# Expert search of two PEER layers issued in shares per slab behind the low parts, with GpSimd's low parts and the gate steps placed differently

## The chip, the cores and the metric

One core of one Trainium2 chip runs the whole kernel in one launch. Times are device microseconds (us). The engines are TensorE (PE, weight loads PEld), VectorE (DVE), ScalarE (ACT), GpSimd (POOL) and SyncE (SP, which issues the loads). The time before is the median of three runs, 2640.13 us (2637.69 to 2642.39).

## The reference, cut to what matters

Eight stages follow each other over 256 tokens of width 1024, all in float32: an MLA mixer, a PEER layer, a DSA mixer, a second PEER layer, and two pairs of hybrid mixer and SwiGLU. Each ends in a layernorm. The change is in the two PEER layers:

```python
q = (xt @ w_q).reshape(T, PEER_HEADS, 2, PEER_QDIM // 2)
s1 = jnp.einsum('thd,hnd->thn', q[:, :, 0], sub_keys[0])
s2 = jnp.einsum('thd,hnd->thn', q[:, :, 1], sub_keys[1])
v1, i1 = lax.top_k(s1, PEER_TOPK)
v2, i2 = lax.top_k(s2, PEER_TOPK)
cand = (v1[..., :, None] + v2[..., None, :]).reshape(T, PEER_HEADS, 256)
best, pos = lax.top_k(cand, PEER_TOPK)
expert = jnp.take_along_axis(cand_idx, pos, axis=-1)
gate = jax.nn.softmax(best, axis=-1)
# per token, over its 8 * 16 experts:
a = x . w_down[expert];  hg = gelu(a) * gate;  y = sum(hg * w_up[expert])
```

Eight heads each choose 16 of 128 x 128 = 16,384 experts.

## The kernel before, in words

The kernel gathers no expert rows. It multiplies all tokens with all 16,384 rows of w_down, slab by slab (128 slabs of 128 experts, loop at L959), takes Gelu, multiplies by a gate that is zero for experts that were not chosen, and multiplies the result H with all of w_up (128 slabs, L992).

*Products in parts.* A float32 product is made of three fp32r products. `Stream._split` (L55 to L71) takes each loaded weight tile of 128 x 1024, `raw`, in the order of a written plan; ScalarE makes the high part `whi` (L67), and VectorE, or GpSimd where the plan's third field says so, the low part `wlo` = raw - high (L69). `raw` has four buffers, the parts have three. `Stream.get` for slab k makes the parts up to k + 2 and so lets their loads go out. `mmS` (L191 to L193) then issues 24 matmuls per slab: for each of eight blocks high x high, high x low of x, and low x high. In the plan the odd peer_down slabs under 40 and every fourth one after that have their low part made by GpSimd, 42 of 128 in each layer.

*The search.* While the slabs run, `route()` (L872) works out the choice on VectorE. `keys_of` finds the 16 best of 128 keys per head, side and token half with five instructions (`topk16`, L761: max, max_index, match_replace, max, max_index). `experts_of` builds 54 candidate sums per head (L782) and finds the 16 best of those. `select` (L804) makes the gates: subtract the best, Exp on ScalarE, sum, reciprocal, normalise (L813). `keys16` (L821) turns positions into key numbers with one-hot comparisons and sums of 16-bit numbers (L840 to L843). `to_hk` (L790) transposes the results on PE and writes them, twice over, into IG.

*What sets the order.* The work is written as a generator in `self.bg`, and `tick` advances it by one yield: twice per pair of query slabs (L907), once per down slab (L976). That is only the order in which the program is traced: the scheduler behind Tile (L1356) may move an instruction ahead on its engine when its data is ready, and each engine then runs a fixed order. Nothing ties the search to the low parts.

*The gates.* When the generator is spent, the routing's memory is given back, H1 is opened, and `gates()` (L924) takes over: for eight tokens at a time four 16-bit one-hot operations on VectorE (L939), then after two steps 16 matmuls (L946), whose sum multiplies the H of finished slabs on VectorE (L951) or is copied into H for later ones on ScalarE (L954). Later slabs then take Gelu into `av` and multiply on GpSimd (L974). 32 groups of two steps make 64 steps, one more before them reads the number row and one after them ends it. `drain` after the loop finishes what is left over.

Of the kernel before, what the change touches and what calls it, by code (L numbers as in the profile page):

```python
# [34 lines left out]
class Stream:  # L35
# [21 lines left out]
    def _split(self, upto):  # L57
        nc = self.nc
        while self.splits <= min(upto, len(self.plan) - 1):
            i = self.splits  # L60
            self._load(i)
            w = self.plan[i][1].shape[-1]
            r = self.raws.pop(i)
            pool = self.tail if self.plan[i][3] else self.spl
            hi = pool.tile([128, 1024], F32R, name="whi")
            lo = pool.tile([128, 1024], F32R, name="wlo")
            nc.scalar.activation(hi[:, :w], r[:, :w], AF.Copy)  # L67
            eng = nc.gpsimd if self.plan[i][2] else nc.vector
            eng.tensor_tensor(lo[:, :w], r[:, :w], hi[:, :w].bitcast(F32), ALU.subtract)  # L69
            self.parts[i] = (hi, lo)  # L70
            self.splits += 1  # L71
            self._load(i + self.nraw)
# [20 lines left out]
def make_plan(I, stages):  # L93
    plan = []

    def add(key, ap, pool=False, tail=False):
        plan.append((key, ap, pool, tail))

    for s in stages:
# [17 lines left out]
        elif s[:4] == "peer":  # L117
# [3 lines left out]
            for k in range(12):  # L121
                add("peer_q", I["peer_q"][l, k])
            for k in range(128):
                add("peer_down", I["peer_down"][l, k], k % (2 if k < 40 else 4) == 1)
            for k in range(128):
                add("peer_up", I["peer_up"][l, k], False, k > 123)
        elif s[:3] == "mix":
# [29 lines left out]
class Build:  # L157
# [591 lines left out]
    def peer(self, l):  # L749
        nc, I, st, tc = self.nc, self.I, self.st, self.tc  # L750
        with ExitStack() as c0:
# [6 lines left out]
            P16 = [rp.tile([128, 8, 16], U32, name=f"P{a}") for a in range(2)]  # L758
            best = rp.tile([128, 2, 8, 16], F32, name="best")

            def topk16(vals, idx, src, w):  # L761
                s2 = rp.tile([128, 128], F32, name="s2", bufs=2)
                nc.vector.max(vals[:, 0:8], src)
                nc.vector.max_index(idx[:, 0:8], vals[:, 0:8], src)
                nc.vector.match_replace(s2[:, :w], vals[:, 0:8], src, FLOOR)  # L765
                nc.vector.max(vals[:, 8:16], s2[:, :w])
                nc.vector.max_index(idx[:, 8:16], vals[:, 8:16], s2[:, :w])  # L767

            def keys_of(hd, ss):
                for a in range(2):  # L770
                    for side in range(2):
                        topk16(V[a][:, side, hd], X[a][:, side, hd], ss[:, side, a, :], 128)
                        yield

            def experts_of(h0, a):

                w = int(CSTART[-1])
                hs = slice(h0, h0 + 4)
                cd = rp.tile([128, 4, w], F32, name="cand", bufs=2)
                for (i, n, m), o in zip(CAND, (int(CSTART[c[0]]) for c in CAND)):  # L780
                    sh = [128, 4, n, m]
                    nc.vector.tensor_tensor(cd[:, :, o:o + n * m].rearrange("p h (i j) -> p h i j", i=n),  # L782
                                            V[a][:, 0, hs, i:i + n, None].to_broadcast(sh),
                                            V[a][:, 1, hs, None, 0:m].to_broadcast(sh), ALU.add)
                for j in range(4):
                    topk16(best[:, a, h0 + j], P16[a][:, h0 + j], cd[:, j], w)
                    if j != 1:
                        yield

            def to_hk(src, j, a):  # L790

# [11 lines left out]

            def select():  # L804

                e = rp.tile([128, 16, 16], F32, name="ge")
                gs = rp.tile([128, 2, 16], F32, name="gs")
                bv = best.rearrange("p a h k -> p (a h) k")
                nc.vector.tensor_tensor(e, bv, bv[:, :, 0:1].to_broadcast([128, 16, 16]), ALU.subtract)
                nc.scalar.activation(e, e, AF.Exp)  # L810
                nc.vector.reduce_sum(gs[:, 0], e, AX.X)
                nc.vector.reciprocal(gs[:, 1], gs[:, 0])
                nc.vector.tensor_tensor(e, e, gs[:, 1, :, None].to_broadcast([128, 16, 16]), ALU.mult)  # L813
                yield
                for a in range(2):
                    to_hk(e[:, a * 8:a * 8 + 8].rearrange("p a b -> p (a b)"), 2, a)
                yield
                for a in range(2):
                    yield from keys16(a)

            def keys16(a):  # L821

# [9 lines left out]
                dx = rp.tile([128, 8, 16], F16, name="dx")  # L832
                nc.vector.tensor_copy(dx[:, :, 0:1], x16[:, 0, :, 0:1])
                tt(dx[:, :, 1:16], x16[:, 0, :, 1:16], x16[:, 0, :, 0:15], ALU.subtract)
                hot = rp.tile([128, 128, 16], F16, name="hot")
                prod = rp.tile([128, 128, 16], F16, name="prod")

                def total(x, out):

                    tt(prod.rearrange("p (h k) i -> p h k i", h=8), hot.rearrange("p (h k) i -> p h k i", h=8), x, ALU.mult)  # L840
                    for n in (8, 4, 2):
                        tt(prod[:, :, 0:n], prod[:, :, 0:n], prod[:, :, n:2 * n], ALU.add)
                    tt(out, prod[:, :, 0:1], prod[:, :, 1:2], ALU.add)  # L843

                lists = lambda x: x[:, :, None, :].to_broadcast([128, 8, 16, 16])
                tt(duo(hot), pos[:, :, None, :].to_broadcast(R), row(1), ALU.is_ge)
                yield
                k1 = rp.tile([128, 128, 1], F32, name="k1")
                total(lists(dx), k1)
                yield  # L850
                first = rp.tile([128, 128, 1], F16, name="first")
                total(self.rows16[:, 2, None, None, :].to_broadcast([128, 8, 16, 16]), first)
                yield
                to_hk(k1.rearrange("p k u -> p (k u)"), 0, a)
                tt(pos, pos, first.to_broadcast([128, 128, 2]), ALU.subtract)
                tt(duo(hot), pos[:, :, None, :].to_broadcast(R), row(0), ALU.is_equal)
                yield
                k2 = rp.tile([128, 128, 1], F32, name="k2")
                total(lists(x16[:, 1]), k2)
                yield  # L860
                yield
                to_hk(k2.rearrange("p k u -> p (k u)"), 1, a)

            def scores_of(hd, qT, ss):
                b = self.acc()
# [6 lines left out]
            def route():  # L872
# [86 lines left out]
            for k in range(128):  # L959
# [5 lines left out]
                if k % 2:  # L965
# [394 lines left out]
```

## Time and profile before

| | us |
|---|---|
| median of three runs | 2640.13 |
| profiled execution, its own time | 2644.85 |
| its span, first to last instruction | 2643.1 |
| PE busy | 2596.4 (98%) |
| DVE busy | 1826.4 (69%) |
| ACT busy | 1366.8 (52%) |
| POOL busy | 433.9 (16%) |

The two peer_down loops lie at 157 to 568 us and 1107 to 1520 us of the span. Busy time of PE is no measure of its speed, since matmuls overlap; the number of matmuls in a stretch is. A slab is 24 matmuls.

### The profile page before, as it was taken

The numbers are of one execution on the slowest core, as the hardware profiler recorded it, in microseconds if no ns is written. First come the engines' busy times: TensorE is split into PE (matmuls) and PEld (weight loads), VectorE is DVE, ScalarE is ACT, GpSimd is POOL, SyncE is SP. The second block draws the span as 40 slices with busy tenths as digits, with TensorE's granted clock in tenths as the row PEclk, the third lists the DMA queues.
The fourth block names the chain that finished last, engine by engine and source line by source line (L and its number), as shares of the span: only waits on it lengthen the run. The fifth ranks groups of instructions, "written<-read, shape, count | busy, mean of one in ns | idle before, by whom it ended". The sixth has DMA issues, their size and how long they took to land.

```text
span 2643.1 us, 44763 instructions
## 1 busy us (share of the span) xinstructions
PE 2596.4 (98%) x17412; PEld 2374.2 (90%) x17412; DVE 1826.4 (69%) x3301; ACT 1366.8 (52%) x2091; POOL 433.9 (16%) x292
## 2 busy tenths in 40 slices
PE   8999999999999999989999999999999999999998
PEld 7899999998888887989999988888899899899898
DVE  6696689956666688885799666666766655666555
ACT  5544454455555555544544455555576444575443
POOL 1024333430000032133234400000101000101000
PEclk9999999999999999999999999999999999999999
DMA  5555545566676655545555566766645666536664
GB/s 196 185 152 165 181 155 159 157 185 193 192 225 195 193 187 176 158 153 172 174 159 153 175 191 193 228 193 192 215 126 177 223 189 208 181 121 207 208 186 141
DMA packets 134213, 477.05 MB, mean 180 GB/s; under 512 B 15568, under 2 KB 17376, under 8 KB 133744
## 3 DMA queue, kind: packets, MB, share of 16 engines
q1 hardware_dynamic: 130016, 459.43, 55.7%
q0 software_dynamic: 3984, 14.76, 1.5%
q8 instruction: 136, 2.23, 0.4%
q14 instruction: 77, 0.63, 0.1%
HBM read 465.74 MB, written 8.39 MB: 179 GB/s over the span
## 4 chain that ended last, share of the span: by engine, by line
PE 70%; issue 15%; DVE 10%; DMA 2%; ACT 1%; POOL 1%; SPq 0%; DVEq 0%; POOLq 0%; ACTq 0%
PE acc L202 20%; PE acc L199 10%; PE wk L191 9%; PE wk L193 9%; PE wk L192 9%; PE acc L946 2%; DVE wlo L69 2%; PE acc L191 2%; PE acc L192 2%; PE acc L193 2%; PE acc L241 1%; DVE xres L353 1%; DVE s L765 1%; DVE X L767 1%; DVE z L362 1%
## 5 line engine op out<-in xcount | busy, mean ns | idle before, releaser
L69 DVE TENSOR_TENSOR wlo<-raw,whi 128x1024 fp32r<-128x1024 f32 (+2 forms) x766 | 947.0, 1240 | 553.0 <-ACT whi L67 541.4
L67 ACT ACTIVATE whi<-raw 128x1024 fp32r<-128x1024 f32 (+3 forms) x854 | 895.4, 1051 | 709.7 <-PE wk L192 346.4
L193 PE MATMUL wk<-xTh,wlo 128*128 128x256 f32 x2880 | 818.5, 284 | 14.7 <-DVE wlo L69 14.7
L191 PE MATMUL wk<-xTh,whi 128*128 128x256 f32 x2880 | 824.4, 286 | 0.0
L192 PE MATMUL wk<-xTl,whi 128*128 128x256 f32 x2880 | 817.0, 284 | 0.0
L193 PEld LDWEIGHTS wk<-xTh,wlo 128*128 128x128 f32 x2880 | 554.7, 193 | 16.5 <-DVE wlo L69 16.1
L191 PEld LDWEIGHTS wk<-xTh,whi 128*128 128x128 f32 x2880 | 554.6, 193 | 2.1 <-ACT whi L67 0.9
L192 PEld LDWEIGHTS wk<-xTl,whi 128*128 128x128 f32 x2880 | 554.9, 193 | 1.4
L202 PE MATMUL acc<-wlo,hgh 128*128 128x512 f32 x1024 | 315.9, 389 | 0.0
L202 PE MATMUL acc<-whi,hgl 128*128 128x512 f32 x1024 | 315.7, 389 | 0.1
L69 POOL TENSOR_TENSOR wlo<-raw,whi 128x1024 fp32r<-128x1024 f32 x88 | 227.3, 2584 | 359.5 <-ACT whi L67 351.2
L199 PE MATMUL acc<-whi,hgh 128*128 128x512 f32 x1024 | 276.0, 389 | 0.0
L254 ACT ACTIVATE hgh<-H 128x256 fp32r<-128x256 f32 x256 | 106.4, 418 | 288.1 <-PE acc L202 288.0
L202 PEld LDWEIGHTS acc<-whi,hgl 128*128 128x128 f32 x1024 | 192.1, 188 | 40.4 <-DVE hgl L255 0.5
L202 PEld LDWEIGHTS acc<-wlo,hgh 128*128 128x128 f32 x1024 | 192.2, 188 | 39.9
L199 PEld LDWEIGHTS acc<-whi,hgh 128*128 128x128 f32 x1024 | 192.1, 188 | 39.9
L255 DVE TENSOR_TENSOR hgl<-H,hgh 128x256 fp32r<-128x256 f32 x256 | 111.8, 439 | 114.6 <-PE acc L202 114.2
L974 POOL TENSOR_TENSOR H<-H,av 128x512 f32<-128x512 f32 (+16 forms) x76 | 103.5, 1361 | 271.1 <-ACT av L973 258.3
L356 POOL TENSOR_TENSOR lsm<-lsm,mhalf 128x1 f32<-128x1 f32 x16 | 9.0, 562 | 838.9 <-DVE lsm L355 484.7
L191 PE MATMUL acc<-xTh,whi 128*128 128x256 f32 x384 | 112.0, 292 | 0.0
L193 PE MATMUL acc<-xTh,wlo 128*128 128x256 f32 x384 | 110.0, 287 | 0.0
L192 PE MATMUL acc<-xTl,whi 128*128 128x256 f32 x384 | 109.1, 284 | 0.0
(412 smaller groups left out, 3442.9 us busy)
## 6 DMA issues: line engine op xcount, KB each, us to landing
raw<-in_peer_down SPq DMA_DIRECT2D x256, 512.0 KB, 3.6
raw<-in_peer_up SPq DMA_DIRECT2D x256, 512.0 KB, 4.2
raw<-in_ffn_down SPq DMA_DIRECT2D x44, 512.0 KB, 4.2
raw<-in_ffn_gate SPq DMA_DIRECT2D x40, 512.0 KB, 4.2
raw<-in_ffn_up SPq DMA_DIRECT2D x40, 512.0 KB, 4.2
raw<-in_peer_q SPq DMA_DIRECT2D x32, 512.0 KB, 4.2
raw<-in_gates SPq DMA_DIRECT2D x32, 512.0 KB, 3.5
raw<-in_dsa_qkv SPq DMA_DIRECT2D x24, 512.0 KB, 4.5
```

What stands on the lines that cost most here:

```text
L67: nc.scalar.activation(hi[:, :w], r[:, :w], AF.Copy)
L69: eng.tensor_tensor(lo[:, :w], r[:, :w], hi[:, :w].bitcast(F32), ALU.subtract)
L191: mm(out, whi[:, sl[k]], xh[:, k, :], start=k == 0, stop=False)
L192: mm(out, whi[:, sl[k]], xl[:, k, :], start=False, stop=False)
L193: mm(out, wlo[:, sl[k]], xh[:, k, :], start=False, stop=k == nk - 1)
L199: mm(o, xh, whi[:, c], start=first, stop=False)
L202: self.last_mm = mm(o, x, w[:, c], start=False, stop=s)
L241: mm(o, xh, w[:, c], start=s, stop=False)
L254: nc.scalar.activation(hi, src, AF.Copy)
L255: nc.vector.tensor_tensor(lo, src, hi.bitcast(F32), ALU.subtract)
L946: nc.tensor.matmul(b[:, j * 128:j * 128 + 128], B[:, 4 * q + j], A[:, 4 * q + j], start=first and j == 0, stop=not first and j == 3)
L974: nc.gpsimd.tensor_tensor(H[j][:, c, :n], H[j][:, c, :n], av[:, :, :n], ALU.mult)
```

## The change

Five edits, all within the two PEER layers.

1. GpSimd makes the low parts of the odd down slabs under 24 only: 12 per layer instead of 42.
2. `_split` remembers the last low part that VectorE makes (`last_lo`).
3. The search yields after every VectorE instruction or a few of them, with a number for its cost. A new function `pace` takes over from `tick`: each call adds a share to the account (1850 while heads and candidates are ranked, 1200 from `select` on, 850 more per call in the query stage) and issues steps until it is used up. All that it issues is placed after `last_lo` on VectorE.
4. The transposes (`to_hk`) are put in a list, `later`, and issued at the fourth call of `pace` counted from the one that made their data, and the gate's normalisation follows the first step of `keys16`.
5. The gates step in every slab but those divisible by 6.

```diff
             eng = nc.gpsimd if self.plan[i][2] else nc.vector
-            eng.tensor_tensor(lo[:, :w], r[:, :w], hi[:, :w].bitcast(F32), ALU.subtract)
+            ins = eng.tensor_tensor(lo[:, :w], r[:, :w], hi[:, :w].bitcast(F32), ALU.subtract)
+            if not self.plan[i][2]:
+                self.last_lo = ins
...
-                add("peer_down", I["peer_down"][l, k], k % (2 if k < 40 else 4) == 1)
+                add("peer_down", I["peer_down"][l, k], k < 24 and k % 2 == 1)
...
             def topk16(vals, idx, src, w):
                 s2 = rp.tile([128, 128], F32, name="s2", bufs=2)
+                cost = 120 + w
                 nc.vector.max(vals[:, 0:8], src)
+                yield cost
                 nc.vector.max_index(idx[:, 0:8], vals[:, 0:8], src)
+                yield cost
...
                 nc.scalar.activation(e, e, AF.Exp)
-                nc.vector.reduce_sum(gs[:, 0], e, AX.X)
-                nc.vector.reciprocal(gs[:, 1], gs[:, 0])
-                nc.vector.tensor_tensor(e, e, gs[:, 1, :, None].to_broadcast([128, 16, 16]), ALU.mult)
-                yield
-                for a in range(2):
-                    to_hk(e[:, a * 8:a * 8 + 8].rearrange("p a b -> p (a b)"), 2, a)
-                yield
-                for a in range(2):
-                    yield from keys16(a)
+                share = 1200
+                yield 400
+                for x in keys16(0):
+                    yield x
+                    if e is not None:
+                        nc.vector.reduce_sum(gs[:, 0], e, AX.X)
+                        nc.vector.reciprocal(gs[:, 1], gs[:, 0])
+                        nc.vector.tensor_tensor(e, e, gs[:, 1, :, None].to_broadcast([128, 16, 16]), ALU.mult)
+                        for a in range(2):
+                            turn(e[:, a * 8:a * 8 + 8].rearrange("p a b -> p (a b)"), 2, a)
+                        e = None
+                        yield 800
+                yield from keys16(1)
+
+            def turn(*args):
+                later.append([4, args])
...
                     tt(prod.rearrange("p (h k) i -> p h k i", h=8), hot.rearrange("p (h k) i -> p h k i", h=8), x, ALU.mult)
+                    yield 1000
                     for n in (8, 4, 2):
                         tt(prod[:, :, 0:n], prod[:, :, 0:n], prod[:, :, n:2 * n], ALU.add)
+                        yield 120 + n * 60
                     tt(out, prod[:, :, 0:1], prod[:, :, 1:2], ALU.add)
+                    yield 250
...
+            search, later, spent, share = route(), [], 0, 1850
+
+            def pace(more=0):
+
+                nonlocal search, spent
+                spent -= share + more
+                with tc.issue_after(st.last_lo.ins):
+                    while search and spent < 0:
+                        c = next(search, None)
+                        if c is None:
+                            search = None
+                        else:
+                            spent += c
+                    for x in later:
+                        x[0] -= 1
+                    while later and later[0][0] <= 0:
+                        to_hk(*later.pop(0)[1])
...
-            self.bg = [route()]
...
                 if hd > 2:
-                    self.tick(2)
+                    pace(850)
...
-                self.tick()
-                if not self.bg and not routed:
+                if routed:
+                    if k % 6:
+                        self.tick()
+                else:
+                    pace()
+                if not routed and not search and not later:
                     routed = True
```

The costs in the steps left out are 130 for a candidate sum, 800 for the start of `keys16`, 1000 for its first comparison and 1300 for its second.

## Rows read from the trace of the kernel before

**Rows 1.** The page, busy time of each engine: us, share of the span, instructions

```profile
PE 2596.4 (98%) x17412; PEld 2374.2 (90%) x17412; DVE 1826.4 (69%) x3301; ACT 1366.8 (52%) x2091; POOL 433.9 (16%) x292
```

**Rows 2.** The table of waits: who <- for whom: us in total, times, longest

```profile
PE wk L193 <- DVE wlo L69: 14.7, 7, 3.0
```

**Rows 3.** Windows: stretch, us, busy PE PEld DVE ACT POOL (instructions), clock, DMA

```profile
163.71:192.51 28.80, 28.80 (x243) 28.80 (x241) 28.80 (x177) 14.30 (x16) 11.27 (x5) 1.00 0.55 165
192.51:228.81 36.30, 28.41 (x219) 27.60 (x217) 36.06 (x91) 14.71 (x17) 12.86 (x5) 0.95 0.42 129
231.69:257.61 25.92, 25.92 (x219) 25.92 (x217) 7.79 (x7) 11.96 (x14) 10.52 (x5) 1.00 0.59 187
453.02:520.09 67.07, 67.07 (x643) 66.64 (x641) 66.90 (x93) 31.27 (x59) 29.87 (x16) 1.00 0.52 157
1142.85:1180.61 37.76, 30.97 (x218) 30.36 (x217) 37.52 (x92) 14.72 (x17) 11.55 (x5) 0.86 0.41 138
```

**Rows 4.** Timeline at a wait of PE, layer 0: start, us, instruction, [idle before]

```profile
190.84 2.39 POOL L69 TENSOR_TENSOR wlo<-raw,whi 128x1024 fp32r<-128x1024 f32 x1 [3.36 <-ACT whi L67]
190.97 2.31 DVE L782 TENSOR_TENSOR cand<-V 128x32 f32<-128x32 f32 x1
193.60 1.21 DVE L69 TENSOR_TENSOR wlo<-raw,whi 128x1024 fp32r<-128x1024 f32 x1
194.87 0.39 PE L193 MATMUL wk<-xTh,wlo 128*128 128x256 f32 x1 [1.96 <-DVE wlo L69]
```

**Rows 5.** Timeline of VectorE in the search, layer 0

```profile
160.11 0.87 DVE L763 MAX8 V<-ss 128x8 f32<-128x128 f32 x4
162.08 0.07 DVE L764 MATCH_VALUE_LOAD X<-V,ss 128x8 f32 x1
162.34 0.07 DVE L764 MATCH_VALUE_LOAD X<-V,ss 128x8 f32 x1
```

**Rows 6.** Search operations by line: ns least/median/most, first to last start

```profile
L766 DVE MAX8 V<-s x64: 268/284/304, 134.3 to 1139.9; 128x8 f32<-128x128 f32 x64
L767 DVE FIND_INDEX8 X<-V,s x64: 278/289/303, 137.7 to 1143.6; 128x8 uint32<-128x128 f32 x64
L782 DVE TENSOR_TENSOR cand<-V x40: 172/196/2308, 141.5 to 1143.8; 128x32 f32<-128x32 f32 x16, 128x40 f32<-128x40 f32 x8, 128x48 f32<-128x48 f32 x8, 128x64 f32<-128x64 f32 x8
```

**Rows 7.** High parts (L67) and low parts (L69) by line

```profile
L67 ACT ACTIVATE whi<-raw x854: 634/1060/1070, 5.5 to 2622.4; 128x1024 fp32r<-128x1024 f32 x168, 128x704 fp32r<-128x704 f32 x2, 128x584 fp32r<-128x584 f32 x1
L69 DVE TENSOR_TENSOR wlo<-raw,whi x766: 681/1225/3417, 6.3 to 2623.5; 128x1024 fp32r<-128x1024 f32 x187, 128x704 fp32r<-128x704 f32 x2, 128x584 fp32r<-128x584 f32 x2, 128x768 fp32r<-128x768 f32 x1
L69 POOL TENSOR_TENSOR wlo<-raw,whi x88: 2383/2406/4478, 154.5 to 1506.7; 128x1024 fp32r<-128x1024 f32 x88
```

**Rows 8.** Timeline of ScalarE around Exp, layer 0

```profile
202.18 1.28 ACT L810 ACT_TABLE_LOAD   x1
206.66 0.42 ACT L810 ACTIVATE ge<-ge 128x256 f32<-128x256 f32 x1 [3.20 <-DVE ge L809]
208.99 1.28 ACT L970 ACT_TABLE_LOAD   x1
```

**Rows 9.** Groups of VectorE, 192.51 to 228.81: xcount | busy us, mean ns

```profile
L813 DVE TENSOR_TENSOR ge<-ge,gs 128x256 f32<-128x256 f32 x1 | 2.6, 2635 | 0.0
L842 DVE TENSOR_TENSOR prod<-prod 128x1024 f16<-128x1024 f16 x3 | 2.0, 680 | 0.0
L842 DVE TENSOR_TENSOR prod<-prod 128x512 f16<-128x512 f16 x3 | 1.2, 415 | 0.0
L840 DVE TENSOR_TENSOR prod<-hot,x 128x2048 f16<-128x2048 f16 x1 | 1.2, 1224 | 0.0
```

**Rows 10.** Gate operations by line: ns least/median/most

```profile
L939 DVE TENSOR_TENSOR A<-io,IG x64: 675/682/2897, 283.0 to 1473.2; 128x1024 f16<-128x1024 f16 x64
L951 DVE SCALAR_TENSOR_TENSOR H<-acc,H x228: 155/396/426, 322.5 to 1483.1; 128x256 f32<-128x256 f32 x102, 128x208 f32<-128x208 f32 x2, 128x216 f32<-128x216 f32 x2, 128x224 f32<-128x224 f32 x2
L974 POOL TENSOR_TENSOR H<-H,av x76: 315/1401/2173, 327.4 to 1521.6; 128x512 f32<-128x512 f32 x14, 128x16 f32<-128x16 f32 x2, 128x32 f32<-128x32 f32 x2, 128x48 f32<-128x48 f32 x2
```

More of the change, by code (lines that the diff above doesn't have):

```diff
@@ L762, in topk16 @@
                 s2 = rp.tile([128, 128], F32, name="s2", bufs=2)
+                cost = 120 + w
                 nc.vector.max(vals[:, 0:8], src)
+                yield cost
                 nc.vector.max_index(idx[:, 0:8], vals[:, 0:8], src)
+                yield cost
                 nc.vector.match_replace(s2[:, :w], vals[:, 0:8], src, FLOOR)
+                yield cost
                 nc.vector.max(vals[:, 8:16], s2[:, :w])
+                yield cost
                 nc.vector.max_index(idx[:, 8:16], vals[:, 8:16], s2[:, :w])
+                yield cost
             def keys_of(hd, ss):
@@ L771, in keys_of @@
                     for side in range(2):
-                        topk16(V[a][:, side, hd], X[a][:, side, hd], ss[:, side, a, :], 128)
-                        yield
+                        yield from topk16(V[a][:, side, hd], X[a][:, side, hd], ss[:, side, a, :], 128)
             def experts_of(h0, a):
@@ L784, in experts_of @@
                                             V[a][:, 1, hs, None, 0:m].to_broadcast(sh), ALU.add)
+                    yield 130
                 for j in range(4):
-                    topk16(best[:, a, h0 + j], P16[a][:, h0 + j], cd[:, j], w)
-                    if j != 1:
-                        yield
+                    yield from topk16(best[:, a, h0 + j], P16[a][:, h0 + j], cd[:, j], w)
             def to_hk(src, j, a):
@@ L804, in select @@
             def select():
+                nonlocal share
                 e = rp.tile([128, 16, 16], F32, name="ge")
@@ L810, in select @@
                 nc.scalar.activation(e, e, AF.Exp)
-                nc.vector.reduce_sum(gs[:, 0], e, AX.X)
-                nc.vector.reciprocal(gs[:, 1], gs[:, 0])
-                nc.vector.tensor_tensor(e, e, gs[:, 1, :, None].to_broadcast([128, 16, 16]), ALU.mult)
-                yield
-                for a in range(2):
-                    to_hk(e[:, a * 8:a * 8 + 8].rearrange("p a b -> p (a b)"), 2, a)
-                yield
-                for a in range(2):
-                    yield from keys16(a)
+                share = 1200
[13 more added lines that the diff above has]
+                later.append([4, args])
             def keys16(a):
@@ L834, in keys16 @@
                 tt(dx[:, :, 1:16], x16[:, 0, :, 1:16], x16[:, 0, :, 0:15], ALU.subtract)
+                yield 800
                 hot = rp.tile([128, 128, 16], F16, name="hot")
@@ L840, in total @@
                     tt(prod.rearrange("p (h k) i -> p h k i", h=8), hot.rearrange("p (h k) i -> p h k i", h=8), x, ALU.mult)
+                    yield 1000
                     for n in (8, 4, 2):
                         tt(prod[:, :, 0:n], prod[:, :, 0:n], prod[:, :, n:2 * n], ALU.add)
+                        yield 120 + n * 60
                     tt(out, prod[:, :, 0:1], prod[:, :, 1:2], ALU.add)
+                    yield 250
                 lists = lambda x: x[:, :, None, :].to_broadcast([128, 8, 16, 16])
                 tt(duo(hot), pos[:, :, None, :].to_broadcast(R), row(1), ALU.is_ge)
-                yield
+                yield 1000
                 k1 = rp.tile([128, 128, 1], F32, name="k1")
-                total(lists(dx), k1)
-                yield
+                yield from total(lists(dx), k1)
+                turn(k1.rearrange("p k u -> p (k u)"), 0, a)
                 first = rp.tile([128, 128, 1], F16, name="first")
-                total(self.rows16[:, 2, None, None, :].to_broadcast([128, 8, 16, 16]), first)
-                yield
-                to_hk(k1.rearrange("p k u -> p (k u)"), 0, a)
+                yield from total(self.rows16[:, 2, None, None, :].to_broadcast([128, 8, 16, 16]), first)
                 tt(pos, pos, first.to_broadcast([128, 128, 2]), ALU.subtract)
                 tt(duo(hot), pos[:, :, None, :].to_broadcast(R), row(0), ALU.is_equal)
-                yield
+                yield 1300
                 k2 = rp.tile([128, 128, 1], F32, name="k2")
[L859 to L862, printed above, removed]
+                yield from total(lists(x16[:, 1]), k2)
+                turn(k2.rearrange("p k u -> p (k u)"), 1, a)
             def scores_of(hd, qT, ss):
```

## The prediction

> **What bounds the kernel now.** The page first: TensorE (PE) is busy 98% of the span [rows 1], so only what makes it wait, or run at half clock, can be won. The table of waits comes second. One wait of PE stands out: the third product of a slab waits for a low part that VectorE (DVE) makes, 14.7 us in 7 waits [rows 2]. Third, the windows say where. In the peer_down loop of layer 0, 10 undisturbed slabs (240 matmuls) take 28.80 us, 2.88 us each; the next 9 take 36.30 us, and in layer 1 the corresponding 9 take 37.76 us instead of 25.92 [rows 3]. The excess is 36.30 - 25.92 = 10.4 us and 37.76 - 25.92 = 11.8 us, **22.2 us** in all. That is more than the 14.7 us of waiting, because the granted clock averages 0.95 and 0.86 in those two windows and 1.00 in all others: the other 7.5 us is work at the lower level, half of the 2.4 GHz, after PE had stood. In the same windows DVE is busy 36.06 of 36.30 us; a little later, 7.79 of 25.92 us. The gate stretch (453 to 520 us) has DVE busy 66.90 of 67.07 us, and PE does not wait there at all [rows 3]. So DVE is not short of time over the loop: the expert search is crowded into slabs 2 to 20.
>
> Fourth, the timeline shows how one wait arises. At 192.91 us PE stops for 1.96 us; DVE began a candidate sum at 190.97 that lasted 2.31 us and only then, after three short instructions, made the low part at 193.60 [rows 4]. A candidate sum takes 0.196 us as a rule [rows 6]. It was long because GpSimd (POOL) was making a low part at that time (started 190.84, 2.39 us) [rows 4]. The gate normalisation (`ge`) took 2.635 us in the same stretch [rows 9]. POOL suffers in turn: up to 4.478 us against a median of 2.406 [rows 7].
>
> **The change, part by part.**
>
> *Instruction counts.* No matmul, activation or transfer is added or removed; 30 low parts per layer (42 odd ones before, 12 after) move from POOL to DVE. That is 30 x 1.225 us = 37 us of DVE per layer [rows 7].
>
> *Slack of a low part.* Three buffers, so slab k+2's high part may start when slab k-1 has been multiplied, two slabs or 5.76 us before it is needed. High part 1.060 us plus DVE low part 1.225 leaves 3.4 us; with POOL's 2.406, 2.3 us [rows 7]. A search share that delays a low part by less costs nothing.
>
> *Search, slabs 0 to 22.* Counting the generator's costs, the five calls of the query stage issue 13,500 units, then each slab 1,850, and the ranking of candidates ends at k = 22. Each share stands behind the last DVE-made low part, so two shares lie between the low parts of two even slabs. One top-16 of 128 keys is 1,240 units. Its real price has two ends. Neighbours that don't depend on each other overlap: four MAX8 in 0.87 us, so 0.20 each though one lasts 0.28, and a load-plus-index pair every 0.26 us [rows 5]; that gives 0.20 + 0.26 + 0.26 + 0.20 + 0.26 = 1.18 us. End to end by durations, a load 0.07 to 0.08 and its partner 0.29: 0.284 + 0.366 + 0.36 + 0.284 + 0.366 = 1.66 us [rows 5, 6]. I take 1.18, since a pair of shares holds three top-16s that can alternate as the two do now. Then two shares cost 2 x 1,850 / 1,240 x 1.18 = 3.5 us, plus a low part 1.2: 4.7 of 5.76 us. A candidate block that meets POOL adds about 2.1 us; four blocks per layer, two slabs apart at the least, which lie within the 1.0 us per slab pair that is left plus the slack of 3.4. Stall: 0.
>
> By the Trainium skill, VectorE: DVE Perf Modes, "The DRAIN you can't avoid", the next operation does not start until the pipe is empty, which is the 1.66 us end. The MAX8 row disagrees where the neighbours are independent; no row here shows a strictly dependent chain of them. By that page the sum would be the first rival's.
>
> *Search, slabs 23 to 40.* 1,200 units per slab. A product takes 1.224 us, the first add 0.680, the second 0.415 and the last two about as much: 3.2 us for 2,450 units [rows 9]; a comparison has as many elements as the product and counts 1,000. At that rate a share is 1.5 us, plus a low part 1.22: 2.7 of 2.88 us. Tight, but the biggest single share (k = 37: adds, sum, subtraction and a comparison) is 2.9 us, and delays the next low part by 2.9 + 1.2 - 2.88 = 1.2 us, under 3.4. POOL has no low part any more, so I use the undisturbed durations, and the normalisation should shrink. A cost that stays: ScalarE's Exp has a table load of 1.28 us before it and one after it, takes 0.42, and waited 3.20 us for DVE in layer 0 [rows 8]. Together 6.2 us in the way of the high parts against a slack of 3.4, so between 0 and 2.8 us per layer; the wait should shrink with smaller shares ahead of it, so I take 0.5, which is 1.0 in both layers.
>
> *Transposes.* They come four calls after their sums, some three slabs; PE meets data that is ready. By the account, routing ends at k = 44 instead of 48.
>
> *Gates.* 66 steps at 5 of 6 slabs from k = 45 put the last gate matmul after k = 123 (before: one per slab from 49 to 114). Four slabs, 11.5 us, remain there to hide the last multiplications before peer_up. Six slabs take 6 x 2.88 + 2.5 groups x 0.95 = 19.65 us (the gate pair 6.71 against 5.76, from 10 pairs in 67.07 us [rows 3]). DVE's need: four one-hot operations of 0.68 (the first by its median, the others alike) and two large and two small multiplications, 0.40 and some 0.25 (an estimate between their least and their median) [rows 10]: 4.0 us a group, 2.5 x 4.0 + 6 x 1.225 = 17.4 us. Stall: 0. The other end is what a group costs today, beside POOL's low parts: ten groups and 15 low parts fill 66.90 us [rows 3], so a group at most (66.90 - 15 x 1.225) / 10 = 4.85 us, and six slabs 2.5 x 4.85 + 7.35 = 19.5 us, which still fits.
>
> *Sum.* The profiled execution took 2644.85 us (span 2643.1), 4.7 above the median 2640.13. It becomes 2644.85 - 22.2 + 1.0 = 2623.7; off the median, 2640.13 - 21.2 = **2619 us**, 0.8% faster.
>
> **The rivals.**
>
> *Part of the stall stays.* If the shares run end to end, two cost 2 x 1,850 / 1,240 x 1.66 = 4.95 + 1.22 = 6.2 us, 0.4 over 5.76; 11.5 pairs give 4.8 us, two candidate blocks that meet POOL 4.2, less 3.4 of slack: 5.6 us per layer, 11.2 in both. That is 2640.1 - 22.2 + 11.2 = 2629, and with lower clock after the waits in the present proportion (22.2 / 14.7), 2635. For it: a top-16's five steps depend on each other. Against: DVE alternates two chains today, and is full for 28.80 us of slabs 2 to 11 without a wait of PE [rows 3].
>
> *Nothing is won.* All four blocks meet POOL as well: 4.8 + 8.4 - 3.4 = 9.8 per layer, 2638 us. Or the scheduler's order under the new constraint leaves a low part behind a long share as often as now.
>
> *Slower: the gate stretch runs out of DVE.* Its place is slabs 46 to 123, where DVE now makes every low part. POOL's products of H, about three per six slabs, take 1.40 us (up to 2.17) [rows 10] and may block DVE for their whole length. It decides when a group costs DVE more than (19.65 - 7.35) / 2.5 = 4.92 us. With three full blocks of 1.40 six slabs need 17.4 + 4.2 = 21.6 us, 1.95 too much; over 13 such stretches, less 3.4 of slack, 22 us per layer, and 2640 - 22 + 44 = 2662. With 2.17 it is 2722. For it: DVE is full there now, and loses the help of POOL. Against: it is full with a group every 2 slabs, which now comes every 2.4, and the 4.85 us already hold POOL's products and five of its low parts besides.
>
> **How the numbers follow.** The forecast has 0.70, its own range 2615 to 2624 (below, all of the stall gone and the 2.4 us by which the lowest of the runs lies under the median; above, the Exp term in full). Partial stall 0.16, nothing won 0.07, gates slower 0.07. What a measurement tells from no change here is about 0.2%, 5.3 us, so below 2634.9 is faster: 0.70 and most of 0.16 give 0.85; same 0.08; slower 0.07. The range 2614 to 2634 takes in the forecast and most of the partial case.
>
> **What would show it.** Right: the wait of PE for low parts falls from 14.7 us in 7 waits to under 2; every slab from k = 2 on takes 2.88 us (3.8 where gates or transposes are between); the clock stays at 1.00 through both loops; POOL has 24 + 4 low parts instead of 88; the normalisation well under 2.6 us; DVE about 80 to 95% busy through slabs 0 to 40 instead of full and then idle; the last gate matmul nine slabs later in the loop. Wrong: PE waits for low parts spread through slabs 3 to 22 (first rival), around slab 24 after Exp, or from slab 46 on (the slower case), with DVE near full there.

## The result, and the profile after

The changed kernel takes 2618.47 us (median of 4 runs, 2617.39 to 2620.39) against 2640.06 us (4 runs): ratio 0.9915, 95% interval 0.9903 to 0.9926. The forecast was 2619.

The profiled execution of the changed kernel has a span of 2615.6 us, 27.5 less than before. 5.8 us of that lie ahead of the first PEER layer's query products (they start at 107.7 us, before at 113.5), in code that the change does not touch; they are no part of its gain. The medians differ by 21.6 us, and the two loops account for that: from the first slab's start to the last slab's they take 397.85 us each, before 408.19 and 409.65, together 22.1 us less.

First the page, engine busy times, as in [rows 1]; then the three waits of PE that lasted longest in total, as in [rows 2].

```profile
PE 2586.2 (99%) x17412; PEld 2366.5 (90%) x17412; DVE 1812.8 (69%) x3361; ACT 1362.3 (52%) x2103; POOL 258.3 (10%) x234
```

```profile
PE acc L201 <- ACT whi L67: 6.2, 1, 6.2
PE wk L308 <- DVE z L364: 4.0, 8, 0.8
PE wk L449 <- ACT PT L443: 3.5, 5, 0.9
```

The wait of the third slab product (now L195) for `wlo`, 14.7 us before, is no longer in the table: the three above lie at the start, in layernorms and in attention. The windows over the same slabs as the first two of [rows 3], and one of equal length in the gate stretch (columns as there):

```profile
157.92:186.72 28.80, 28.80 (x243) 28.80 (x241) 23.25 (x143) 14.30 (x16) 11.28 (x5) 1.00 0.59 181
186.72:212.64 25.92, 25.92 (x219) 25.92 (x217) 21.03 (x114) 11.96 (x14) 10.32 (x5) 1.00 0.59 177
451.05:518.12 67.07, 67.07 (x634) 66.68 (x633) 60.27 (x88) 31.67 (x58) 12.70 (x11) 1.00 0.52 160
```

The nine slabs that took 36.30 us take 25.92, at a clock of 1.00 instead of 0.95. DVE is busy 81% of slabs 2 to 20, where it was full. In the gate stretch it went from 66.90 to 60.27 of 67.07 us, although it makes every low part there; but that window holds nine groups of gates, not ten (144 gate matmuls instead of 160), because the gates step more slowly.

The timeline of DVE and POOL over two shares (start, us, instruction, what ended the idle time before it) answers to [rows 4]:

```profile
159.14 1.23 DVE L69 TENSOR_TENSOR wlo<-raw,whi 128x1024 fp32r<-128x1024 f32 x1 [2.58 <-ACT whi L67]
160.68 0.64 DVE L790 TENSOR_TENSOR cand<-V 128x64 f32<-128x64 f32 x5
162.04 2.41 POOL L69 TENSOR_TENSOR wlo<-raw,whi 128x1024 fp32r<-128x1024 f32 x1 [4.27 <-ACT whi L67]
...
164.90 1.22 DVE L69 TENSOR_TENSOR wlo<-raw,whi 128x1024 fp32r<-128x1024 f32 x1 [1.14 <-ACT whi L67]
166.52 0.64 DVE L790 TENSOR_TENSOR cand<-V 128x64 f32<-128x64 f32 x5
167.78 2.40 POOL L69 TENSOR_TENSOR wlo<-raw,whi 128x1024 fp32r<-128x1024 f32 x1 [3.32 <-ACT whi L67]
```

DVE's low parts come 5.76 us apart, two slabs. The five candidate sums stand near the head of the share, 0.3 to 0.4 us behind the low part, and are over 0.6 to 0.7 us before POOL starts. POOL then works beside the search's instructions with one input (MAX8, FIND_INDEX8, MATCH_REPLACE8 and their loads, 6 to 19 of them per low part). None of its 24 low parts for the down slabs overlaps a VectorE operation with two inputs. The rows by line show what that does to the durations in the whole run (ns least/median/most, as in [rows 6, 7] and, for `ge`, [rows 9]; the last row is one of the search instructions with one input, 296 ns at most):

```profile
L790 DVE TENSOR_TENSOR cand<-V x40: 182/194/221, 160.7 to 1152.6; 128x32 f32<-128x32 f32 x16, 128x64 f32<-128x64 f32 x8, 128x40 f32<-128x40 f32 x8, 128x48 f32<-128x48 f32 x8
L826 DVE TENSOR_TENSOR ge<-ge,gs x2: 419/420/420, 228.7 to 1168.2; 128x256 f32<-128x256 f32 x2
L69 POOL TENSOR_TENSOR wlo<-raw,whi x28: 2379/2402/2483, 148.7 to 1153.4; 128x1024 fp32r<-128x1024 f32 x28
L775 DVE FIND_INDEX8 X<-V,s x64: 281/286/296, 126.4 to 1147.6; 128x8 uint32<-128x128 f32 x64
```

The longest candidate sum went from 2308 to 221 ns, the normalisation from 2635 to 420, POOL's longest low part from 4478 to 2483. Around Exp on ScalarE, as in [rows 8]:

```profile
222.97 1.28 ACT L818 ACT_TABLE_LOAD   x1
224.26 0.42 ACT L818 ACTIVATE ge<-ge 128x256 f32<-128x256 f32 x1
```

Exp follows its table load at once; before, it waited 3.20 us for DVE.

So the profile alone would let one write that spreading the search cured the crowding. The experiments say otherwise.

### The profile page after: what moved, and what is told of

It reads as the page before. It is cut to its first block, busy times and chain, and to the rows that moved or that the text cites. A ratio compares the mean times of both kernels' runs of the same rounds, so it can differ in the third digit from the quotient of the medians.

```text
span 2615.6 us, 44686 instructions
## 1 busy us (share of the span) xinstructions
PE 2586.2 (99%) x17412; PEld 2366.5 (90%) x17412; DVE 1812.8 (69%) x3361; ACT 1362.3 (52%) x2103; POOL 258.3 (10%) x234
## 4 chain that ended last, share of the span: by engine, by line
PE 76%; issue 15%; DVE 4%; DMA 2%; ACT 1%; POOL 1%; SPq 0%; DVEq 0%; POOLq 0%; ACTq 0%
PE acc L204 21%; PE wk L193 11%; PE wk L195 11%; PE wk L194 11%; PE acc L201 10%; PE acc L978 2%; PE acc L193 2%; PE acc L194 2%; PE acc L195 2%; PE acc L243 1%; DVE wlo L69 1%; DVE xres L355 1%; ACT whi L67 1%; POOL mg L1229 1%; DVE z L364 1%
## 5 line engine op out<-in xcount | busy, mean ns | idle before, releaser
L69 DVE TENSOR_TENSOR wlo<-raw,whi 128x1024 fp32r<-128x1024 f32 (+2 forms) x826 | 1005.3, 1220 | 520.3 <-ACT whi L67 508.2
L67 ACT ACTIVATE whi<-raw 128x1024 fp32r<-128x1024 f32 (+3 forms) x854 | 895.6, 1052 | 742.5 <-PE wk L194 346.1
L195 PE MATMUL wk<-xTh,wlo 128*128 128x256 f32 x2880 | 814.7, 283 | 0.0
L195 PEld LDWEIGHTS wk<-xTh,wlo 128*128 128x128 f32 x2880 | 551.8, 192 | 0.2
L1006 POOL TENSOR_TENSOR H<-H,av 128x80 f32<-128x80 f32 (+31 forms) x78 | 87.2, 1118 | 591.3 <-ACT av L1005 591.3
L195 PE MATMUL acc<-xTh,wlo 128*128 128x256 f32 x384 | 110.0, 287 | 0.0
L983 DVE SCALAR_TENSOR_TENSOR H<-acc,H 128x256 f32<-128x256 f32 (+19 forms) x228 | 73.7, 351 | 40.5 <-PE acc L978 40.4
L201 PE MATMUL acc<-whi,xTh 128*128 128x512 f32 (+3 forms) x268 | 91.6, 382 | 6.9 <-ACT whi L67 6.2
```

The lines of the kernel that those rows point to most:

```text
L69: ins = eng.tensor_tensor(lo[:, :w], r[:, :w], hi[:, :w].bitcast(F32), ALU.subtract)
L195: mm(out, wlo[:, sl[k]], xh[:, k, :], start=False, stop=k == nk - 1)
L201: mm(o, xh, whi[:, c], start=first, stop=False)
L983: nc.vector.scalar_tensor_tensor(H[j][:, c, t], bv[:, g], 1.0 / GS, H[j][:, c, t], op0=ALU.mult, op1=ALU.mult)
```

## The experiments

The theory on record was that the search, crowded into the first slabs, stands in front of low parts. The rival that proved to matter is that GpSimd's low parts make VectorE's operations long. The eleven kernels, each against the kernel before in the same session (median 2641 to 2642 us; 2640 for the changed kernel); GpSimd's operations are given per layer:

| kernel | search | GpSimd's down low parts | us | ratio, 95% interval |
|---|---|---|---|---|
| before | free | odd under 40, then every 4th | 2641 | 1 |
| e1 | free | odd under 24 | 2640.0 | 0.9997 (0.9987 to 1.0006) |
| e10 | free | as before from 27 on | 2618.9 | 0.9912 (0.9895 to 0.9929) |
| e7 | free | none | 2617.9 | 0.9912 (0.9894 to 0.9929) |
| e9 | free | none; 12 useless subtractions | 2643.6 | 1.0011 (1.0001 to 1.0020) |
| e11 | free | none; 24 useless fills | 2618.9 | 0.9914 (0.9897 to 0.9930) |
| e4 | shares, no edge | odd under 24 | 2641.7 | 1.0000 (0.9991 to 1.0010) |
| e8 | shares, no edge | none | 2619.1 | 0.9917 (0.9899 to 0.9935) |
| e2 | shares and edge | as before | 2635.5 | 0.9978 (0.9969 to 0.9988) |
| changed | shares and edge | odd under 24 | 2618.5 | 0.9915 (0.9903 to 0.9926) |
| e5 | shares and edge | none | 2619.8 | 0.9917 (0.9899 to 0.9934) |
| e3 | as changed, gates in every slab | odd under 24 | 2618.8 | 0.9912 (0.9896 to 0.9929) |
| e6 | as changed, shares doubled | odd under 24 | 2696.7 | 1.0212 (1.0193 to 1.0230) |

### e1: the plan alone

```diff
-                add("peer_down", I["peer_down"][l, k], k % (2 if k < 40 else 4) == 1)
+                add("peer_down", I["peer_down"][l, k], k < 24 and k % 2 == 1)
```

> The kernel before with the plan of the change alone: GpSimd makes 12 low parts per layer, all in the slabs below 24; the search and the gates are stepped as before. My theory (the search, moved ahead by the scheduler into slabs 2 to 20, stands in front of low parts on VectorE) says that the stall stays, because in those slabs nothing is changed: about 14 us of PE waiting for low parts and about 22 us of excess in slabs 12 to 20, median 2635 to 2645 us. In the gate stretch VectorE now makes every low part with a group every 2 slabs: 4.0 + 2 x 1.225 = 6.45 of 6.71 us, so no new wait; by the dearer group of today, 4.85 + 2.45 = 7.3 of 6.71, it would be up to 2670. The rival (GpSimd's low parts are what lengthens VectorE's operations, so fewer of them is the cure) says 2618 to 2625.

2640.0 us. The waits are in slabs 12, 16, 18 and 20 of both layers, as in layer 0 before; in total (who waits for whom: us, times, longest):

```profile
PE wk L193 <- DVE wlo L69: 15.7, 8, 3.1
```

As expected. It does not yet separate the two causes, since GpSimd's low parts are unchanged in just those slabs. It shows that the gate stretch bears all low parts on DVE even with a group every two slabs: PE does not wait there. DVE is even busy for less time. Slabs 60 to 99 with 20 groups, first the kernel before, then this one (columns as in [rows 3]):

```profile
345.71:479.85 134.14, 134.14 (x1283) 133.28 (x1281) 125.84 (x182) 66.55 (x123) 49.42 (x31) 1.00 0.51 158
342.31:476.44 134.13, 134.13 (x1282) 133.27 (x1281) 117.18 (x194) 66.81 (x124) 25.11 (x20) 1.00 0.51 158
```

DVE makes all 40 low parts instead of 30, about 12 us of work more, and is busy 8.7 us less: the ten low parts on GpSimd cost DVE more than they saved it. Before, each of the ten lengthened an operation of the gates, to 2.4 to 2.7 us, and PE did not wait even so.

### e2: the change without its plan

```diff
-                add("peer_down", I["peer_down"][l, k], k < 24 and k % 2 == 1)
+                add("peer_down", I["peer_down"][l, k], k % (2 if k < 40 else 4) == 1)
```

> The changed kernel with the old plan: GpSimd again makes 42 low parts per layer, 20 of them below slab 40; shares, order and gate steps stay as changed. Theory: the shares behind the low parts carry the gain. In slabs 24 to 40 nine GpSimd low parts can lengthen a 16-bit operation by about 1.8 us each; two shares 3.0 + low part 1.22 + 1.8 = 6.0 of 5.76 us, 0.3 per slab pair, under 3 us in all and inside the slack of 3.4. 2617 to 2624 us, no PE wait for low parts above 2 us in all; candidate sums or normalisation near 2 us may reappear. Rival (the plan carries it): 2630 to 2640.

2635.5 us, 17 us above the changed kernel: the expectation missed, and the time lies in the rival's range. Slabs 2 to 20 are as in the changed kernel, 28.80 and 25.92 us; PE waits in slabs 30, 34 and 38 of each layer. The timeline around the last of these in layer 0:

```profile
264.84 2.76 POOL L69 TENSOR_TENSOR wlo<-raw,whi 128x1024 fp32r<-128x1024 f32 x1 [3.14 <-ACT whi L67]
265.25 2.90 DVE L971 TENSOR_TENSOR Bh<-E,IG 128x1024 f16<-128x1024 f16 x1
268.07 0.68 DVE L971 TENSOR_TENSOR Bl<-E,IG 128x1024 f16<-128x1024 f16 x1
268.67 1.21 DVE L69 TENSOR_TENSOR wlo<-raw,whi 128x1024 fp32r<-128x1024 f32 x1
...
269.94 0.39 PE L195 MATMUL wk<-xTh,wlo 128*128 128x256 f32 x1 [3.04 <-DVE wlo L69]
```

A gate operation, `Bh`, began 0.4 us after a GpSimd low part and lasted 2.90 us instead of 0.68; PE waited 3.04 us for the low part behind it. The expectation had counted the search's own operations only. The gates of the first token half had been moved ahead into slabs where the search still runs, and no edge binds them. For the waits in slabs 30 and 34 the held operation was VectorE's own low part (3.41 and 3.42 us), which had not been counted either.

### e3: gates in every slab

```diff
                 if routed:
-                    if k % 6:
-                        self.tick()
+                    self.tick()
```

> The changed kernel with the gates stepping in every slab again, not in 5 of 6. Theory: VectorE needs 4.0 + 2 x 1.225 = 6.45 us per pair of slabs of 6.71, so PE still does not wait: 2616 to 2622 us, VectorE 93 to 97% busy in the gate stretch. Rival (VectorE runs out there, so the slower stepping is needed): 7.3 of 6.71 us, 0.6 too much per pair, 32 pairs, less 3.4 of slack, about 15 us per layer, 2640 to 2650 us with PE waiting for low parts between slabs 46 and 114.

2618.8 us, as expected: PE does not wait in either loop. DVE is busy 117.37 of 134.13 us in slabs 60 to 99, 88%, below the 93 to 97% expected. The stepping in 5 of 6 slabs is worth nothing that can be measured.

### e4: the change without its order edge

```diff
-                with tc.issue_after(st.last_lo.ins):
+                with nullcontext():
```

> The changed kernel without the order edge: the shares are traced per slab as in the change, but their instructions are not placed behind the last low part. Theory: the scheduler moves them ahead again, VectorE is full in slabs 2 to 20 and then idle, and PE waits for low parts there: 2630 to 2640 us, 8 us or more of such waits. Rival (the even shares in the traced order are enough): 2617 to 2621 us, VectorE 75 to 85% busy in slabs 2 to 20, no wait.

2641.7 us: everything is lost. PE waits in slabs 12, 18 and 20 of both layers. But the timeline shows GpSimd in it again, at the normalisation of layer 0; the total of the waits first:

```profile
PE wk L195 <- DVE wlo L69: 13.6, 6, 3.0
...
208.43 2.39 POOL L69 TENSOR_TENSOR wlo<-raw,whi 128x1024 fp32r<-128x1024 f32 x1 [1.41 <-ACT whi L67]
208.47 2.63 DVE L826 TENSOR_TENSOR ge<-ge,gs 128x256 f32<-128x256 f32 x1
```

DVE began 0.04 us after POOL, and the operation that takes 0.42 us in the changed kernel lasted 2.63. The time is on the side of the theory of crowding, 1.7 us above its range, and fits the rival as well. Hence the next kernels, without GpSimd.

### e7: the kernel before, VectorE makes every down low part

```diff
-                add("peer_down", I["peer_down"][l, k], k % (2 if k < 40 else 4) == 1)
+                add("peer_down", I["peer_down"][l, k], False)
```

> The kernel before with no down low part on GpSimd and nothing else changed: no shares, no order edge, gates in every slab. Theory now (the stall comes from VectorE operations that GpSimd's low parts lengthen by about 2 us each, 4 to 6 per layer, behind which a low part stands in a fixed order that does not allow for it): no long candidate sum, normalisation or product is left, and PE's waits for low parts go from 14.7 us to under 3, 2618 to 2624 us, although the search is still crowded into the first slabs. Rival (crowding: without an order edge the search stands in front of low parts whatever its length, and VectorE now has 20 more low parts to make there): 2635 to 2660 us.

2617.9 us: one line earns all that the change earns. The windows over slabs 2 to 11 and 12 to 20 of layer 0 (columns as in [rows 3]):

```profile
157.82:186.62 28.80, 28.80 (x243) 28.80 (x241) 28.80 (x152) 14.33 (x16) 0.00 (x0) 1.00 0.60 181
186.62:212.54 25.92, 25.92 (x219) 25.92 (x217) 25.92 (x121) 13.21 (x15) 0.00 (x0) 1.00 0.58 185
```

DVE is busy without a gap for 54.72 us, the search is as crowded as it was, and PE does not wait once. Crowding alone is not the cause.

### e8: shares without the edge, and no GpSimd

```diff
-                add("peer_down", I["peer_down"][l, k], k < 24 and k % 2 == 1)
+                add("peer_down", I["peer_down"][l, k], False)
...
-                with tc.issue_after(st.last_lo.ins):
+                with nullcontext():
```

> The changed kernel without the order edge and with no down low part on GpSimd; only the shares as traced and the 5 of 6 gate steps are left of the change. Theory (lengthened operations are the cause): 2617 to 2623 us, as the changed kernel. Rival (the edge is what keeps the low parts ahead): 2635 us or more, with PE waiting in slabs 12 to 20 as without the edge alone.

2619.1 us, no wait. With e4 it is the clean pair: the same shares without an edge take 2641.7 us with 12 GpSimd low parts per layer and 2619.1 without.

### e5: the change with every down low part on VectorE

```diff
-                add("peer_down", I["peer_down"][l, k], k < 24 and k % 2 == 1)
+                add("peer_down", I["peer_down"][l, k], False)
```

> The changed kernel with no down low part on GpSimd: VectorE makes all 128 per layer, shares and order edges as changed. The two shares between two low parts took 3.4 us in the changed kernel, so one share 1.7, plus a low part of 1.14 to 1.22: 2.84 to 2.92 us of 2.88 per slab. At most 0.04 x 21 slabs, 1 us, too much, inside the slack of 3.4: no wait, 2617 to 2621 us, VectorE 97 to 100% busy in slabs 2 to 20. Rival (the 12 low parts on GpSimd are needed there): 2624 us or more.

2619.8 us, no wait, DVE full to 98 and 99% in the windows of slabs 2 to 11 and 12 to 20:

```profile
158.97:187.77 28.80, 28.80 (x243) 28.80 (x242) 28.18 (x143) 14.33 (x16) 0.00 (x0) 1.00 0.59 181
187.77:213.69 25.92, 25.92 (x219) 25.92 (x218) 25.76 (x122) 11.96 (x14) 0.00 (x0) 1.00 0.59 183
```

So GpSimd's 12 low parts are not needed either.

### e9: useless GpSimd subtractions beside a cured kernel

```diff
-            eng = nc.gpsimd if self.plan[i][2] else nc.vector
+            eng = nc.gpsimd if self.plan[i][2] is True else nc.vector
             eng.tensor_tensor(lo[:, :w], r[:, :w], hi[:, :w].bitcast(F32), ALU.subtract)
+            if self.plan[i][2] == 2:
+                nc.gpsimd.tensor_tensor(self.junk[:, :w], r[:, :w], hi[:, :w].bitcast(F32), ALU.subtract)
...
-                add("peer_down", I["peer_down"][l, k], k % (2 if k < 40 else 4) == 1)
+                add("peer_down", I["peer_down"][l, k], 2 if k < 24 and k % 2 == 1 else False)
...
+            st.junk = rp.tile([128, 1024], F32, name="junk")
```

> The kernel before with every down low part made by VectorE (2618 us), plus 12 useless GpSimd subtractions per layer: the low parts of the odd slabs under 24 are made a second time, into a tile that nobody reads. Theory (a GpSimd operation that runs beside a two-input VectorE operation lengthens it, and low parts stand behind it): VectorE operations of 2 to 3 us are back in slabs 10 to 22, three to six per layer, and PE waits for VectorE's low parts again, 6 to 16 us in all: 2628 to 2645 us. Rival (low parts made by GpSimd come late, or buffers come free late, and the neighbourhood of the two engines is harmless): no PE wait, 2617 to 2622 us.

2643.6 us: 12 operations per layer that nobody waits for cost 26 us. PE's waits, 19.9 us, are above the 6 to 16 expected. The wait table, and the timeline around one wait:

```profile
PE wk L195 <- DVE wlo L69: 19.9, 16, 1.6
```

```profile
187.26 2.39 POOL L71 TENSOR_TENSOR junk<-raw,whi 128x1024 f32<-128x1024 f32 x1 [2.52 <-ACT whi L67]
187.38 3.36 DVE L69 TENSOR_TENSOR wlo<-raw,whi 128x1024 fp32r<-128x1024 f32 x1
...
190.79 0.38 PE L195 MATMUL wk<-xTh,wlo 128*128 128x256 f32 x1 [1.52 <-DVE wlo L69]
```

POOL ended at 189.65; DVE's low part, begun 0.12 us after POOL, ended 1.1 us later than that, nearly its whole undisturbed time of 1.225. So it stood almost still while POOL worked. The high part was there when POOL began, so no late buffer explains this wait. One thing differs from the expectation: nearly all the lengthened operations here are low parts themselves, nine against one sum of the search in layer 0. Both engines read the same high part; here they start within 0.12 us of each other.

### e11: fills instead of subtractions

The edit is shown against e9.

```diff
-                nc.gpsimd.tensor_tensor(self.junk[:, :w], r[:, :w], hi[:, :w].bitcast(F32), ALU.subtract)
+                t = nc.gpsimd.tensor_copy(self.junk[:, 0:1], hi[:, 0:1].bitcast(F32))
+                with self.tc.issue_after(t.ins):
+                    for _ in range(2):
+                        nc.gpsimd.memset(self.junk[:, :w], 0.0)
```

> As the kernel with the useless subtractions, but GpSimd reads only one column of the high part and then fills the unread tile with zeros twice: about as long an occupation, nearly without reading. The Trainium skill, SBUF - State Buffer, section Who interferes with whom, says that a VectorE operation with two inputs is held only by a GpSimd operation that reads. By it no long candidate sum or product and 2617 to 2622 us; if writing holds VectorE as reading does, the long operations and 2628 to 2645 us.

2618.9 us, no PE wait in the loops and no DVE operation above 1.5 us in slabs 0 to 45 of layer 0. A low part beside a pair of fills, then by line POOL's fills and DVE's candidate sums (ns least/median/most):

```profile
186.12 1.97 POOL L74 MEMSET junk<- 128x1024 f32 x2
186.17 1.21 DVE L69 TENSOR_TENSOR wlo<-raw,whi 128x1024 fp32r<-128x1024 f32 x1
...
L74 POOL MEMSET junk<- x48: 952/955/962, 149.8 to 1157.3; 128x1024 f32 x48
...
L788 DVE TENSOR_TENSOR cand<-V x40: 172/202/246, 136.4 to 1137.5; 128x32 f32<-128x32 f32 x16, 128x40 f32<-128x40 f32 x8, 128x48 f32<-128x48 f32 x8, 128x64 f32<-128x64 f32 x8
```

Two fills and the copy occupy POOL for 2.1 us (2 x 0.955 + 0.185), the subtraction 2.4. DVE's low part began 0.05 us after the first fill and took 1.21 us, as if alone. Each of the twelve odd slabs of layer 0 has a low part of VectorE beside a fill, 1.24 us at most. Occupation by fills does not hold VectorE; the subtraction, which reads, does.

### e10: GpSimd's low parts only from slab 27 on

```diff
-                add("peer_down", I["peer_down"][l, k], k % (2 if k < 40 else 4) == 1)
+                add("peer_down", I["peer_down"][l, k], k > 25 and k % (2 if k < 40 else 4) == 1)
```

> The kernel before, with GpSimd's low parts left out only in slabs up to 25; from 27 on the old plan (7 odd slabs under 40, then every fourth). The search, unpaced, is over by about slab 21, so GpSimd no longer meets it; in the gate stretch it still does, and long operations were there before without a wait. Theory: 2617 to 2622 us, no PE wait for low parts. If the search or the gates moved ahead meet GpSimd in slabs 27 to 40, single waits of 1.5 to 3 us there: up to 2630. Rival (any GpSimd low part in the loop costs): 2630 to 2640.

2618.9 us, no wait. The search was not over by slab 21, as the expectation had it, and two operations of it meet GpSimd low parts, in slabs 25 and 27:

```profile
226.32 2.81 POOL L69 TENSOR_TENSOR wlo<-raw,whi 128x1024 fp32r<-128x1024 f32 x1 [122.61 <-ACT whi L67]
226.79 2.50 DVE L831 CAST x<-X 128x256 f16<-128x256 uint32 x1
...
232.07 2.63 POOL L69 TENSOR_TENSOR wlo<-raw,whi 128x1024 fp32r<-128x1024 f32 x1 [2.94 <-ACT whi L67]
232.46 2.51 DVE L843 TENSOR_TENSOR k<-prod 128x128 f32<-128x128 f16 x1
```

The first is a cast, with one input, which takes 0.29 us undisturbed: two inputs are not the only kind that is held. Neither makes PE wait. That DVE has time to spare there is the likely reason (in the kernel before it was busy 33.73 of 68.50 us from 231.5 us on), but no run tests it.

### e6: double shares

```diff
-                share = 1200
+                share = 2400
...
-            search, later, spent, share = route(), [], 0, 1850
+            search, later, spent, share = route(), [], 0, 3700
```

> The changed kernel with shares twice as large (3700 and 2400), so the search is done in half the slabs. If the shares must be small because a low part waits behind them: two shares 6.8 us plus a low part 1.2 are 8.0 of 5.76 us; over 12 slabs 13 us, less the slack of 3.4, near 10 us of waiting per layer, and as much again in the slabs of the key numbers: 2640 to 2670 us. Rival: the edge only forbids that a share comes before its low part; the scheduler still puts a later low part ahead of what is left of a share, as long as the durations are those it counts on, and then nothing is lost: 2617 to 2622 us.

2696.7 us, on the theory's side and beyond its range. The waits of PE:

```profile
PE wk L195 <- DVE wlo L69: 20.4, 13, 2.5
PE wk L800 <- DVE ge L826: 19.5, 2, 9.8
PE wk L800 <- DVE k L861: 15.4, 2, 8.6
PE acc L201 <- ACT whi L67: 6.3, 1, 6.3
PE wk L195 <- POOL wlo L69: 5.6, 2, 3.7
```

The waits for low parts came as foreseen. What the expectation left out are the transposes: four calls behind their sums is enough at 1200 units per slab, and not when DVE has fallen behind, so PE stood 7 to 10 us before them, four times. Low parts on DVE were held by GpSimd as well (2.7 to 2.95 us in slabs 5, 7 and 9 of layer 0, 3.41 in slab 17). So this run does not price the shares alone.

## Why the prediction was right, and where it was not

*The prize: right.* 22.2 us of excess in the two loops was the forecast, 22.1 went. The signs named for it came too: no wait of PE for low parts, the clock at 1.00 in the windows above, the last gate matmul after slab 123 instead of 114.

*The mechanism: half right, and the time right with some luck.* The prediction named both parts of it, the long operation beside GpSimd and the crowded search, and then put the weight on the second ("DVE is not short of time over the loop: the expert search is crowded"). e7 refutes that as a cause by itself: DVE is as full, and nothing is lost. What the runs show in its place is a hold: a VectorE operation with two inputs in SBUF that starts behind a GpSimd low part makes hardly any headway until POOL is done. It ends 1.8 to 2.2 us late, and a low part behind it in the fixed order is late with it. In layer 0 of the kernel before, such operations lie in slabs 11, 14, 16, 17 and 19 (the last is a low part itself), and PE's waits in slabs 12, 16, 18 and 20. The hold alone is not enough either: in the gate stretch before, held operations of 2.3 to 2.7 us and a DVE busy 66.90 of 67.07 us cost PE no wait. The change removed the contact, and spreading the search was its means and not the cure; that is the luck in a forecast which counted on spreading. e9 brings the waits back with operations that nobody needs, and e11 with write-only ones does not. The Trainium skill, SBUF — State Buffer, "Who interferes with whom", says that a VectorE instruction with two SBUF inputs contends with a GpSimd instruction that reads SBUF and not with one that only writes it, and that the issue order decides who blocks; the traces agree on each point (2.63 us for 0.42 behind a reading low part, a candidate sum of 246 ns at most in the kernel with the fills, and GpSimd's own low part of 4.478 us, begun in slab 13 just after a VectorE low part).

*The role of each edit.* The prediction costed the plan edit as 37 us of DVE, gave it the undisturbed durations from slab 23 on, and credited the shares with the gain. In this change the two are needed together: without the edge (e4) or without the plan (e2), 2641.7 and 2635.5 us. The edge puts the search in step with the low parts, and in the trace its two-input operations then fall between GpSimd's low parts, where without the edge (e4) four of them per layer meet one; the plan keeps GpSimd away from the 16-bit sums. The prediction had not planned this: it let four candidate blocks per layer meet POOL. That a share is also smaller than the time left looks like a condition (e6), and not the gain. The gate edit does nothing measurable (e3).

*Terms of the sum.* Two shares and a low part: 4.7 us predicted; from the low part at 159.14 us to the end of the shares behind it at 163.76 it is 4.6. DVE alternates independent chains, so the end-to-end price of 1.66 us per top-16 did not come, and with it fell the first rival. Candidate blocks that meet POOL, four per layer at 2.1 us: none did. Exp, 1.0 us in both layers: nothing, since DVE was no longer late and its wait of 3.20 us went. These two errors were small: the first was hidden in slack, the second is 1.0 us of the sum.

*Gates.* DVE's need was put at 17.4 of 19.65 us per six slabs, 89%; the window after, with nine groups, says 60.27 of 67.07, 90%. The slower rival fell: GpSimd's products of H lengthen single operations to 1.7 us at most after the change, and there is room for them. The last gate matmul came after slab 123 as counted; the first four came after slabs 39 and 41, before routing ends in the program, since the scheduler may move the first token half's groups ahead.

*What stays open.* Whether another phase of shares and GpSimd low parts would meet again was not tried, and why a held operation makes PE wait in slabs 12 to 20 and not in the gate stretch was not separated. e3, e5, e7, e8, e10, e11 and the changed kernel lie within 2 us of each other; the runs don't rank them, and none of them beats the change by more than the scatter.

## What to carry to other kernels

When an engine waits for VectorE, look for single operations that last several times their median, and at what GpSimd does in that moment; the busy share of VectorE did not tell a harmless crowd from a harmful one. Handing element-wise work to GpSimd to relieve VectorE can cost more than it saves: here 12 subtractions per layer cost 22 to 26 us in all until they were kept out of step with VectorE's two-input operations, and leaving them out was the one-line cure. Before crediting a composite change to its most elaborate part, run its parts one by one and also the plainest kernel that removes the suspected contact.

## What the runs showed of the hardware

A GpSimd subtraction holds a two-input VectorE operation until it is done: 3.36 us for a low part of 1.225 that began 0.12 us after a 2.39 us subtraction. A write-only fill of 128 x 1024 (0.955 us) does not. It holds a VectorE cast with one input too (2.50 us for 0.29 in e10), but not the search's MAX8, FIND_INDEX8 and MATCH_REPLACE8 (0.30 us at most in the changed kernel, beside 24 low parts on GpSimd). And it works both ways: GpSimd's low part took 4.478 us at the most before, and 2.483 once no two-input operation of VectorE met it.
